# Output-weight sums held back during the last two phases of the first product group

## The chip, the cores and the metric

The kernel runs on one core of a Trainium2 chip. The number that counts is the time of one execution in microseconds (us) of device time. The kernel before was run three times; a fourth execution was recorded by the hardware profiler, and its trace is what the profile lines below come from. A core has five engines that follow their own instruction lists and wait for each other through semaphores: TensorE (PE in the profile, with its weight loads as PEld), VectorE (DVE), ScalarE (ACT), GpSimd (POOL) and SyncE (SP), which here issues the DMA transfers and computes nothing.

## The reference, cut to what matters

One layer of a hybrid encoder is computed for 1024 tokens of width 2048. One input projection produces everything that follows; one half of its columns feeds a sparse attention (an indexer scores all keys, each query keeps 256 of them), the other half a Mamba-2 state-space mixer (SSD) behind a short causal convolution. Both results are gated, concatenated and sent through one output projection; a residual and a layer norm close the layer.

```
u = einsum('bsd,de->bse', x, w_in)              # 1024 x 2048 x 6752
q, k, v, z_attn, q_idx, k_idx, w_idx, z_ssd, xbc, dt = split(u)
o_attn = sparse_attention(q, k, v, q_idx, k_idx, w_idx) * silu(z_attn)
o_ssd  = ssd_mixer(xbc, z_ssd, dt)              # conv, scan over chunks, gated RMS norm
mixed  = concatenate([o_attn, o_ssd])           # 1024 x 2048
sub    = einsum('bse,ed->bsd', mixed, w_out)    # 1024 x 2048 x 2048
out    = layer_norm(2 ** 0.25 * x + sub)
```

## The kernel before

**Matrix products.** All large products are float32 in effect: an operand is split into a high and a low part (names `xh` and `xl` for activations, `wh` and `wl` for weights), and three matmuls `xh*wh`, `xl*wh`, `xh*wl` replace one. The split of a weight tile is a pair of instructions: ACT rounds `wh<-wr`, DVE subtracts `wl<-wr,wh`. The same pair, `xh` and `xl`, makes an activation tile.

**Fewer products by Strassen-Winograd.** Both projections are done in 2x2 blocks with seven instead of eight block products, at the price of sums of operand blocks and of result blocks. For the input projection, pairs of column tiles go through such a scheme in two lists, the *product groups* (`PLAN`, `GROUPS`): the first has 8 pairs (keys, values, queries, a part of the SSD input), the second 14. Each group runs in four *phases* (`ph` 0 to 3 in `units`, line 600); a phase goes through all pairs of its group, two at a time, and phases 0 to 2 do so with two pieces for each pair (`f` 0 and 1). A *piece* is 24 matmuls of 512 columns into a PSUM bank `pj`. In phases 0 to 2 the second piece of a pair goes on accumulating on the bank of the first, after an engine has taken the intermediate result out of it: ACT copies it in phase 0 (`t_save`), DVE adds a loaded tile to it in phases 1 and 2 (`t_u`, `t_comb`; the row `u<-pj,u` or `cv<-pj,u`). That second piece cannot begin before (event `after`).

**Activation sets.** Each phase and each `f` multiplies by another set of eight tiles, loaded from DRAM (`xt`, or sums of its blocks, `xf`) and split by `t_xst`. A set can be split only when the tiles of the set two earlier become free, so at such a place eight ACT and eight DVE instructions come close together.

**Sums of the output weights.** For the output projection, four sums T1 to T4 of blocks of `w_out` are needed. They don't depend on the input, and `t_wsum` (line 837) makes them far ahead: 16 rounds, in two tasks of eight (one for each half of the columns). A round loads four 128x512 tiles from `wo` (256 KB each), makes four sums on DVE or GpSimd (`two` picks), and stores them to the DRAM tiles `ts`, 256 KB each. The output projection later loads them as `wr<-ts`.

**What sets the order.** The kernel is written by a planner that runs on the host while the program is built. Side work (everything but the pieces) is split into tasks, Python generators that stop at `Need(...)`: which engines the next step wants, which events, how many free slots of the tile pools (`u` has 29 slots, `keep=6` leaves six of them to others). Between small portions of the pieces, `pump` (line 482) goes through the tasks by priority and lets the first one that `ready` (line 436) accepts place its step. `ready` asks estimated clocks of the engines. So the places of all later instructions depend on what was placed before; a task that is held back leaves its place to others, and the order after it differs as well. Priority 0 belongs to what the pieces need, 5 to the weight sums.

Of the kernel before, what the change touches and what calls it, by code (L numbers as in the profile page):

```python
# [15 lines left out]
D = 2048  # L16
# [74 lines left out]
class Port:  # L91
# [3 lines left out]
    def __init__(self):  # L95
        self.busy = []
# [245 lines left out]


class Need:
    def __init__(self, eng="", ev=(), keep=0, now=False, late=0.0, **slots):
        self.eng, self.ev, self.slots, self.keep, self.now, self.late = eng, ev, slots, keep, now, late


# [7 lines left out]
class Flow:  # L356
# [6 lines left out]
    def __init__(self, nc):  # L363
        self.sim = Sim()
        self.nc = Engines(self, nc)
        self.clk = self.sim.clk
        self.cells = []
        self.tasks = []
        self.pool = {}
        self.slots = {}  # L370
        self.where = {}
        self.n = 0
        self.idle = 0.0
        self.idles = []
        self.spare = 2
        self.pressed = False
        self.first = ("kv10", "kv11", "kv00", "kv01")
        self.spare_u = 9
        self.signals = []
# [56 lines left out]
    def ready(self, task):  # L436
        n = task.need
        if "P" in n.eng:
            now = self.t - self.MARGIN
        else:  # L440
            now = max([self.t] + [self.clk[e] for e in n.eng or ("SP",)]) + 200.0
        late = 0.0 if self.pressed else n.late
        if task.ev.sure(late) + Sim.LAT > (self.t if n.now else now):
            return False
        for e in n.ev:
            if e.t is None or e.sure(late) > now:
                return False
        for tag, k in n.slots.items():
            if self.avail(tag) < k + (min(n.keep, self.spare_u) if tag == "u" else 0):
                return False  # L450
        slack = self.SLACK * (0.5 if task.prio >= 6 else 2 if task.prio == 0 else 1)
        return all(self.clk[e] <= self.t + slack for e in (n.eng or ("D" if task.prio >= 6 else "")) if e != "P")
# [126 lines left out]
class Layer:  # L579
# [20 lines left out]
    def units(self):  # L600

        pieces, work = [], []
        self.hooks = {}
        self.sets = []
        self.mate = {}

        def put(p, listed=True):
            if listed:
                work.append((len(pieces), None))
            pieces.append(p)  # L610
            return len(pieces) - 1

        def plain(h, tile, u, n):
            kind, j = tile
            t = ORDER.index(tile)
            p = Piece("T", h, t, u, load=(("w", t, u),), n=n + u, open=u == 0, close=u == 1, key=(h, t),
                      s0=256 if (kind == "qi" and h == 0) else 0)
            if u == 1:
                p.done = lambda ps: self.fl.add(getattr(self, "t_" + kind)(h, j, ps), 0, f"{kind}{j}h{h}", self.fl.t + 100)
            put(p)  # L620

        for pairs in PLAN:
            if isinstance(pairs, tuple):
                h, tiles, end = pairs
                n = len(self.sets)
                self.sets += [("x", h, 0), ("x", h, 1)]
                for part in [tiles[:3]] + [[t] for t in tiles[3:-end]] + [tiles[-end:]]:
                    for u in range(2):
                        for tile in part:
                            plain(h, tile, u, n)  # L630
                continue
            gi = GROUPS.index(pairs)
            if self.sets[-2:] != [("x", 0, 0), ("x", 0, 1)]:
                self.sets += [("x", 0, 0), ("x", 0, 1)]
            base = len(self.sets) - 2
            self.sets += [("f", "M2"), ("f", "M3"), ("f", "S1"), ("f", "S4"), ("x", 1, 1)]
            couples = [list(range(c, min(c + 2, len(pairs)))) for c in range(0, len(pairs), 2)]
            if len(couples[-1]) == 1:
                couples[-2:] = [couples[-2] + couples[-1]]
            for ph in range(4):  # L640
                for couple in [int(k) if k.isdigit() else k for k in OPENING] if (gi, ph) == (0, 0) else couples:
                    if isinstance(couple, str):
                        tile = ("misc", 0) if couple == "m" else QI["abcdefgh".index(couple)]
                        for u in range(2):
                            plain(0, tile, u, base)
                        continue
                    couple = couples[couple] if isinstance(couple, int) else couple
                    for f in range(1 + (ph < 3)):
                        for c in couple:
                            i = put(self.product(gi, c, pairs[c], ph, f, base + 2 * ph + f))  # L650
                            if f:
                                self.mate[gi, c, ph] = i
                            if ph and (ph, f) != (1, 1):
                                self.hooks.setdefault(max(i - 1, 0), []).append(lambda gi=gi, c=c, ph=ph, f=f: self.pre_ld(gi, c, ph, f))
        end = {}
        for i, p in enumerate(pieces):
            end[p.n] = i
        for i in end.values():
            pieces[i].last = True
        freed = sorted(end, key=end.get)  # L660
        for n in range(2, len(self.sets)):
            at = end[freed[n - 2]] - 2
            self.hooks.setdefault(at, []).append(lambda n=n: self.request(n))
        self.n_t = len(pieces)
        self.hooks.setdefault(self.n_t - 6, []).append(lambda: self.forms(0))
        self.hooks.setdefault(12, []).append(self.form_tasks)
        for half in range(2):
            self.hooks.setdefault(12, []).append(lambda half=half: self.fl.add(self.t_wsum(half), 5, "wsum"))
        for n in range(7):
            for d in range(2):  # L670
                for j in range(4):
                    if n < 6 or 4 * d + j < 8 - SKEW:
                        work.append((len(pieces), (0, 1, 2, 3)))
                    name = PRODUCTS[n][1]
                    pieces.append(Piece("O", n, d, j, load=(("o", name, d, j),)))
        for sts in ((0,), (1,), (2,), (3,)):
            work += [(len(pieces) - SKEW + j, sts) for j in range(SKEW)]
        return pieces, work
# [158 lines left out]
    def t_wsum(self, half):  # L837

        fl = self.fl
        cols = slice(512 * half, 512 * half + 512)  # L840

        def load(name, d, j):
            x = fl.new("us", [P, 512])
            fl.dma(x, self.w_block(name, d, j)[:, cols])
            return x

        def save(name, d, j, x):
            fl.dma(self.tsum[name, d, j][:, cols], x)
        for d in range(2):
            for j in range(4):  # L850
                yield Need("D", u=3, keep=6)
                x, y, z = load("B22", d, j), load("B12", d, j), fl.new("us", [P, 512])
                yield Need("V")
                fl.two(z, x, y, ALU.subtract)
                yield Need("")
                save("T3", d, j, z)
                fl.free(z)
                yield Need("D", us=1)
                z = load("B11", d, j)
                yield Need("V")  # L860
                fl.two(y, y, z, ALU.subtract)
                fl.free(z)
                fl.two(x, x, y, ALU.subtract)
                yield Need("D", us=1)
                save("T1", d, j, y)
                fl.free(y)
                save("T2", d, j, x)
                z = load("B21", d, j)
                yield Need("V")
                fl.two(z, x, z, ALU.subtract)  # L870
                fl.free(x)
                yield Need("")
                save("T4", d, j, z)
                fl.free(z)
                fl.signal(self.ev_wsum[half][4 * d + j])
# [1475 lines left out]
```

## Time and profile before

| | us |
|---|---|
| three runs | 1686.97, 1681.89, 1684.72 |
| median of the three | 1684.72 |
| the profiled execution, whole | 1679.99 |
| its span, first to last instruction | 1677.8 |
| PE busy in the span | 1622.1 (97%) |
| DVE busy | 1324.5 (79%) |
| ACT busy | 1002.2 (60%) |
| DMA, mean share of 16 engines | 71.2% (queue of SP) |

The span is that of one profiled execution; its whole time is 2.2 us longer than the span. In the rows, `out<-in` names what an instruction writes and reads, without the buffers' numbers; a number in square brackets is the idle time of the engine just before it and what ended that idle time. All instructions of the kernel carry the line of one helper (L312), so rows are told apart by tiles. SP rows are DMA issues: `u<-wo` a load, `ts<-u` a store. Matmul rows give a duration of 0.39 us, but they overlap: what counts is the distance from start to start, 0.227 us for 512 columns at full clock. The granted clock of PE is 1.00 or, after some idle stretches, 0.50.

By the order of the matmuls, the third phase of the first group begins at about 427 us of the span, its fourth at 526 us, and the second group at 571 us.

### The profile page before, as it was taken

How to read it: one execution, taken by the hardware profiler on the slowest of the kernel's cores; microseconds unless marked ns; L12 is line 12 of the kernel's file. 1: busy time of each engine (PE TensorE's matmuls, PEld its weight loads, DVE VectorE, ACT ScalarE, POOL GpSimd, SP SyncE). 2: the span in 40 equal slices, each digit the busy share in tenths (PEclk: the TensorE clock that was granted, in tenths of full speed). 3: DMA queues.
4: the chain of work that ended last, by engine and by line, in shares of the span. 5: the costliest groups of instructions: out<-in, count | busy, mean ns of one | idle time of the engine just before them, and what ended most of it. 6: DMA issues, size and time to landing. Idle time of an engine off the chain costs nothing. (4 is left out here: it accounts for less than half of the span.)

```text
span 1677.8 us, 23956 instructions
## 1 busy us (share of the span) xinstructions
PE 1622.1 (97%) x7996; PEld 1341.5 (80%) x7996; DVE 1324.5 (79%) x2437; ACT 1002.2 (60%) x1770; POOL 196.6 (12%) x212
## 2 busy tenths in 40 slices
PE   9999999999998999999999999999999999999997
PEld 6787787888786877888888877888787778888885
DVE  5889998998788876788686668785887676749998
ACT  4555666888877689774445356667757645532330
POOL 0000010000000000104133102312120001100110
PEclk9999999999999999999999999999999989999999
DMA  8177575789789767697684485466878979768654
GB/s 307 54 281 256 183 282 182 274 310 346 262 315 333 267 232 252 206 327 257 218 273 172 156 298 171 158 217 223 290 272 308 328 243 331 235 216 267 228 198 153
DMA packets 192643, 414.48 MB, mean 247 GB/s; under 512 B 19720, under 2 KB 56200, under 8 KB 192520
## 3 DMA queue, kind: packets, MB, share of 16 engines
q1 hardware_dynamic: 192088, 412.56, 71.2%
q8 instruction: 63, 1.03, 0.2%
q14 instruction: 60, 0.49, 0.1%
q10 hardware_dynamic: 432, 0.39, 0.1%
HBM read 308.94 MB, written 103.94 MB: 246 GB/s over the span
## 5 line engine op out<-in xcount | busy, mean ns | idle before, releaser
L312 PE MATMUL pj<-xh,wh 128*128 128x512 f32 (+1 forms) x1496 | 586.3, 392 | 23.2 <-DVE u L312 15.9
L312 PE MATMUL pj<-xh,wl 128*128 128x512 f32 (+1 forms) x1496 | 573.6, 383 | 3.4 <-DVE wl L312 3.4
L312 PE MATMUL pj<-xl,wh 128*128 128x512 f32 (+1 forms) x1496 | 573.3, 383 | 0.2 <-DVE xl L312 0.2
L312 DVE TENSOR_TENSOR wl<-wr,wh 128x1024 fp32r<-128x1024 f32 (+2 forms) x235 | 282.1, 1205 | 187.5 <-ACT wh L312 184.1
L312 PEld LDWEIGHTS pj<-xh,wh 128*128 128x128 f32 x1496 | 283.8, 190 | 78.9 <-issue 18.3
L312 PEld LDWEIGHTS pj<-xh,wl 128*128 128x128 f32 x1496 | 283.3, 189 | 60.9 <-DVE wl L312 5.3
L312 ACT ACTIVATE wh<-wr 128x1024 fp32r<-128x1024 f32 (+2 forms) x242 | 247.8, 1030 | 131.2 <-PE pj L312 100.0
L312 PEld LDWEIGHTS pj<-xl,wh 128*128 128x128 f32 x1496 | 283.9, 190 | 50.2 <-DVE xl L312 1.0
L312 PE MATMUL a<-u,u 128*128 128x512 f32 (+3 forms) x726 | 169.1, 352 | 3.9 <-DVE s L312 2.1
L312 PEld LDWEIGHTS a<-u,u 128*128 128x128 f32 x726 | 119.8, 189 | 37.6 <-DVE s L312 16.0
L312 ACT ACTIVATE u<-s,sm 128x640 bf16<-128x640 int16 (+7 forms) x132 | 129.6, 982 | 31.5 <-DVE sm L312 29.5
L312 DVE TENSOR_TENSOR u<-u,u 128x512 f32<-128x512 f32 (+5 forms) x215 | 139.1, 660 | 3.3 <-DMA u<-wo 0.8
L312 ACT ACTIVATE u<-a 128x512 fp32r<-128x512 f32 (+4 forms) x115 | 53.5, 481 | 147.4 <-PE a L312 74.5
L312 PE MATMUL pj<-wh,xh 128*128 128x512 f32 x318 | 129.5, 407 | 4.8 <-ACT xh L312 4.6
L312 PE MATMUL pj<-wh,xl 128*128 128x512 f32 x318 | 125.2, 394 | 0.1
L312 PE MATMUL pj<-wl,xh 128*128 128x512 f32 x318 | 125.0, 393 | 0.0
L312 ACT ACTIVATE a<-a 128x512 f32<-128x512 f32 (+3 forms) x160 | 77.1, 505 | 65.5 <-PE a L312 62.6
L312 ACT ACTIVATE u<-u 128x512 f32<-128x512 f32 (+4 forms) x147 | 80.6, 557 | 52.9 <-DVE u L312 47.2
L312 DVE TENSOR_TENSOR u<-pj,u 128x512 f32<-128x512 f32 (+2 forms) x112 | 74.6, 667 | 42.1 <-PE pj L312 39.2
L312 DVE TENSOR_TENSOR wr<-wr,wr 128x1024 f32<-128x1024 f32 x80 | 98.8, 1235 | 4.4 <-DMA wr<-wt 4.0
L312 POOL TENSOR_SCALAR s<-s,sm 128x640 f32<-128x640 f32 (+7 forms) x64 | 61.0, 966 | 207.7 <-DVE sm L312 152.5
L312 DVE SCALAR_TENSOR_TENSOR u<-cv,cw,u 128x512 f32<-128x512 f32 x96 | 72.3, 760 | 6.0 <-ACT u L312 3.7
(266 smaller groups left out, 2190.1 us busy)
## 6 DMA issues: line engine op xcount, KB each, us to landing
wr<-wt SPq DMA_DIRECT2D x187, 512.0 KB, 5.1
u<-u SPq DMA_DIRECT2D x110, 256.0 KB, 4.9
wr<-t SPq DMA_DIRECT2D x44, 512.0 KB, 7.6
wr<-ts SPq DMA_DIRECT2D x32, 512.0 KB, 4.9
u<-wo SPq DMA_DIRECT2D x63, 256.0 KB, 5.2
ts<-u SPq DMA_DIRECT2D x63, 256.0 KB, 4.9
s<-xt SPq DMA_DIRECT2D x24, 512.0 KB, 7.6
t<-wr SPq DMA_DIRECT2D x22, 512.0 KB, 2.8
```

Source lines behind the costliest of these rows:

```text
L312: f(*args, **kw)
```

## The change

`Need` gets a mark `rest`; the planner gets a switch `resting`, and `ready` refuses a step so marked while the switch is on. The first step of each round of the weight sums carries the mark. The switch goes on at the first piece of phase 2 (the third) of the first group and off at the first piece of the second group. A round that has begun goes on to its end; no new one begins in between.

```diff
 class Need:
-    def __init__(self, eng="", ev=(), keep=0, now=False, late=0.0, **slots):
+    def __init__(self, eng="", ev=(), keep=0, now=False, late=0.0, rest=False, **slots):
+        self.rest = rest
...
+        self.resting = False
...
     def ready(self, task):
...
+        if n.rest and self.resting:
+            return False
...
             for ph in range(4):
+                if (gi, ph) in ((0, 2), (1, 0)):
+                    self.hooks.setdefault(len(pieces), []).append(lambda on=gi == 0 and ph == 2: setattr(self.fl, "resting", on))
...
     def t_wsum(self, half):
...
-                yield Need("D", u=3, keep=6)
+                yield Need("D", u=3, keep=6, rest=True)
```

The program has as many DMA issues, matmuls and ACT instructions as before; DVE has eight instructions fewer and GpSimd three more; the planner picks the engine of some sums by its clocks. The first 2,088 rows of PE's order are the same; from there on tiles and places differ. By the end of the second group the tasks stand at other points too. Three places follow, each as it stood and as it stands; a name ends in its buffer's and its tile's number.

**SP's queue, about 450 us**, where the first round would have begun. `u<-wo` are loads of the weight sums and `ts` their stores, `u2`, `u3` and `t2` are intermediate results of the first group that come back, `wt` weights of the input projection. Before:

```order
L312 DMA k0_341<-u_806_4540 2x64x512
L312 DMA u_815_4666<-wo 128x512
L312 DMA u_816_4668<-wo 128x512
L312 DMA ts4_02_373<-u_807_4578 128x512
L312 DMA u_824_4705<-u3_0_3_4050 128x512
L312 DMA v0_1_344<-u_812_4595 128x512
L312 DMA u_825_4733<-wo 128x512
L312 DMA u_826_4735<-wo 128x512
L312 DMA wr_830_4742<-t2_0_5_4007 128x1024
L312 DMA wr_831_4743<-wt 128x1024
```

Now:

```order
L312 DMA k0_341<-u_806_4540 2x64x512
L312 DMA ts4_02_373<-u_807_4578 128x512
L312 DMA u_821_4700<-u3_0_3_4050 128x512
L312 DMA v0_1_344<-u_812_4595 128x512
L312 DMA wr_824_4732<-t2_0_5_4007 128x1024
L312 DMA wr_825_4733<-wt 128x1024
```

The four loads are gone from here; the store that remains ends a round begun earlier. From there to the beginning of the second group, ten loads and nine stores of the sums leave SP's queue, and the nine sums between them leave DVE's. The last store of a weight sum stands at place 623 of SP's list, where 582 was.

**DVE's list at the last set change of the third phase, about 508 to 519 us.** `xl` are the low parts of the new set, `wr<-wr,wr` sums of two weight tiles, `wl` the low part of a weight; the last row takes the intermediate result out of the bank of pair 7, and that pair's second piece waits for it. Before:

```order
L312 TENSOR_TENSOR xl_887_5168<-xr_871_5053,xh_886_5167 128x512
L312 TENSOR_TENSOR xl_889_5172<-xr_871_5053,xh_888_5171 128x512
L312 TENSOR_TENSOR wr_875_5093<-wr_875_5093,wr_876_5094 128x1024
L312 TENSOR_TENSOR xl_893_5187<-xr_872_5055,xh_892_5186 128x512
L312 TENSOR_TENSOR xl_895_5197<-xr_872_5055,xh_894_5196 128x512
L312 TENSOR_TENSOR xl_897_5201<-s4_873_5057,xh_896_5200 128x512
L312 TENSOR_TENSOR xl_899_5212<-s4_873_5057,xh_898_5211 128x512
L312 TENSOR_TENSOR xl_901_5216<-s4_874_5059,xh_900_5215 128x512
L312 TENSOR_TENSOR xl_903_5220<-s4_874_5059,xh_902_5219 128x512
L312 TENSOR_TENSOR wl_905_5224<-wr_864_4997,wh_904_5223 128x1024
L312 TENSOR_TENSOR wr_883_5156<-wr_883_5156,wr_884_5157 128x1024
L312 TENSOR_TENSOR u_880_5118<-pj_885_5160,u_880_5118 128x512
```

Now:

```order
L312 TENSOR_TENSOR xl_878_5141<-xr_862_5040,xh_877_5140 128x512
L312 TENSOR_TENSOR xl_880_5145<-xr_862_5040,xh_879_5144 128x512
L312 TENSOR_TENSOR xl_884_5159<-xr_863_5042,xh_883_5158 128x512
L312 TENSOR_TENSOR xl_886_5163<-xr_863_5042,xh_885_5162 128x512
L312 TENSOR_TENSOR wr_868_5083<-wr_868_5083,wr_869_5084 128x1024
L312 TENSOR_TENSOR xl_888_5174<-s4_864_5044,xh_887_5173 128x512
L312 TENSOR_TENSOR xl_890_5178<-s4_864_5044,xh_889_5177 128x512
L312 TENSOR_TENSOR xl_892_5188<-s4_865_5046,xh_891_5187 128x512
L312 TENSOR_TENSOR xl_894_5192<-s4_865_5046,xh_893_5191 128x512
L312 TENSOR_TENSOR wl_896_5197<-wr_856_4978,wh_895_5196 128x1024
L312 TENSOR_TENSOR wr_872_5117<-wr_872_5117,wr_873_5118 128x1024
L312 TENSOR_TENSOR u_871_5094<-pj_876_5133,u_871_5094 128x512
```

The same eight `xl`, two `wr` and one `wl` stand ahead of the last row; what differs is what comes before them in the list, from where the weight sums are gone.

**DVE's list at the last set change of the second group's third phase, about 1206 to 1212 us.** Before:

```order
L312 TENSOR_TENSOR xl_2244_12188<-xr_2205_12008,xh_2243_12187 128x512
L312 TENSOR_TENSOR xl_2246_12192<-xr_2205_12008,xh_2245_12191 128x512
L312 TENSOR_TENSOR wr_2212_12049<-wr_2212_12049,wr_2213_12050 128x1024
L312 TENSOR_TENSOR xl_2248_12203<-s4_2206_12010,xh_2247_12202 128x512
L312 TENSOR_TENSOR xl_2250_12207<-s4_2206_12010,xh_2249_12206 128x512
L312 TENSOR_TENSOR xl_2252_12217<-s4_2207_12012,xh_2251_12216 128x512
L312 TENSOR_TENSOR xl_2254_12221<-s4_2207_12012,xh_2253_12220 128x512
L312 TENSOR_TENSOR wr_2222_12114<-wr_2222_12114,wr_2223_12115 128x1024
L312 TENSOR_TENSOR wl_2259_12232<-wr_2198_11967,wh_2258_12231 128x1024
L312 TENSOR_TENSOR u_2196_11956<-u_2196_11956,u_2224_12124 128x512
L312 TENSOR_TENSOR u_2218_12086<-pj_2237_12159,u_2218_12086 128x512
```

Now:

```order
L312 TENSOR_TENSOR xl_2248_12208<-s4_2205_12017,xh_2247_12207 128x512
L312 TENSOR_TENSOR u_2193_11935<-u_2193_11935,u_2225_12110 128x512
L312 TENSOR_TENSOR u_2182_11876<-a_2250_12214,u_2182_11876 128x256
L312 SCALAR_TENSOR_TENSOR u_2175_11867<-u_2175_11867,dn_222,o_2251_12217 128x256 x2
L312 TENSOR_TENSOR xl_2256_12244<-s4_2206_12019,xh_2255_12243 128x512
L312 TENSOR_TENSOR xl_2258_12248<-s4_2206_12019,xh_2257_12247 128x512
L312 TENSOR_TENSOR wr_2230_12129<-wr_2230_12129,wr_2231_12130 128x1024
L312 TENSOR_TENSOR u_2224_12108<-pj_2235_12163,u_2224_12108 128x512
```

In both, the first row is the first that stands in the program behind the beginning of one piece, and the last is the row that the next piece waits for. Ahead of that last row there were six `xl`, two `wr` sums, a `wl` and a sum of another task; now there are three `xl`, one `wr` sum and four rows of other tasks. The other `xl` stand earlier, the `wl` and a `wr` sum behind.

## The prediction

> **What bounds the kernel now.** I read the page first, then the groups of instructions, then the timeline of PE at its long stops, then DVE, ACT and DMA around those.
>
> ```profile
> span 1677.8 us, 23956 instructions
> PE 1622.1 (97%) x7996; PEld 1341.5 (80%) x7996; DVE 1324.5 (79%) x2437; ACT 1002.2 (60%) x1770; POOL 196.6 (12%) x212
> ```
>
> TensorE is the bound: it is busy 97% of the span, so a change on other engines can give back only what PE loses in stops. The change doesn't touch PE's own work. The gain to be had is therefore read from the stops:
>
> ```profile
> 510.68 0.39 PE L312 MATMUL pj<-xl,wh 128*128 128x512 f32 x1
> 510.90 0.39 PE L312 MATMUL pj<-xh,wl 128*128 128x512 f32 x1
> 519.16 0.77 PE L312 MATMUL pj<-xh,wh 128*128 128x512 f32 x1 [7.87 <-DVE u L312]
> 519.72 0.63 PE L312 MATMUL pj<-xl,wh 128*128 128x512 f32 x1
> 520.15 0.63 PE L312 MATMUL pj<-xh,wl 128*128 128x512 f32 x1
> ...
> 523.06 0.40 PE L312 MATMUL pj<-xh,wh 128*128 128x512 f32 x1
> ...
> 632.56 0.80 PE L312 MATMUL pj<-xh,wh 128*128 128x512 f32 x1 [5.09 <-ACT u L312]
> 997.96 0.77 PE L312 MATMUL pj<-xh,wh 128*128 128x512 f32 x1 [3.11 <-DVE u L312]
> 1212.52 0.77 PE L312 MATMUL pj<-xh,wh 128*128 128x512 f32 x1 [3.15 <-DVE u L312]
> 1344.35 0.80 PE L312 MATMUL pj<-wh,xh 128*128 128x512 f32 x1 [4.64 <-ACT xh L312]
> ```
>
> These five stops, 23.9 us together, are PE's long ones (over 2 us) behind the change's beginning. Three wait for `DVE u`: a second piece cannot begin until DVE has taken the intermediate result out of its bank. A stop also costs clock: behind the one at 519 matmuls start 0.43 us apart (519.72 to 520.15) instead of 0.227, and nine of them start before 523.06, so it costs another 9 x 0.2 = 1.8 us. At 997.96 they start 0.43 apart as well; I put the loss there, and at 1212, at 1.3 us (six or seven matmuls).
>
> **The stop at 519, inside the rest.** These are rows of DVE's timeline up to the one that PE waits for (518.33):
>
> ```profile
> 496.92 1.23 DVE L312 TENSOR_TENSOR wr<-wr,wr 128x1024 f32<-128x1024 f32 x1 [2.60 <-DMA wr<-wt]
> ...
> 502.95 0.69 DVE L312 TENSOR_TENSOR u<-pj,u 128x512 f32<-128x512 f32 x1
> ...
> 507.36 1.23 DVE L312 TENSOR_TENSOR wl<-wr,wh 128x1024 fp32r<-128x1024 f32 x1 [3.38 <-ACT wh L312]
> 508.51 1.29 DVE L312 TENSOR_TENSOR xl<-xr,xh 128x512 fp32r<-128x512 f32 x2
> 510.85 1.23 DVE L312 TENSOR_TENSOR wr<-wr,wr 128x1024 f32<-128x1024 f32 x1 [1.05 <-DMA wr<-wt]
> 511.99 1.29 DVE L312 TENSOR_TENSOR xl<-xr,xh 128x512 fp32r<-128x512 f32 x2
> 513.19 2.49 DVE L312 TENSOR_TENSOR xl<-s,xh 128x512 fp32r<-128x512 f32 x4
> 515.60 1.22 DVE L312 TENSOR_TENSOR wl<-wr,wh 128x1024 fp32r<-128x1024 f32 x1
> 517.19 1.23 DVE L312 TENSOR_TENSOR wr<-wr,wr 128x1024 f32<-128x1024 f32 x1 [0.37 <-DMA wr<-wt]
> 518.33 0.68 DVE L312 TENSOR_TENSOR u<-pj,u 128x512 f32<-128x512 f32 x1
> ```
>
> And one of ACT's:
>
> ```profile
> 498.53 1.05 ACT L312 ACTIVATE u<-s,sm 128x896 bf16<-128x896 f32 x1 [2.30 <-DVE sm L312]
> ```
>
> DVE stood still 3.38 us for ACT's `wh`, and 1.05 and 0.37 us for weights. ACT was late because at 498.53 it had waited 2.30 us for DVE's small rows `sm` of the top-k search, and those stood behind the 2.60 us that DVE waited for a weight at 496.92. So a weight that lands late is passed on twice. Why late:
>
> ```profile
> wr<-wt SPq DMA_DIRECT2D x18, 512.0 KB, 9.2
> wr<-wt SPq DMA_DIRECT2D x187, 512.0 KB, 5.1
> L312 SPq DMA_DIRECT2D ts<-u x10: 320/326/453, 450.5 to 566.2; - x10
> L312 SPq DMA_DIRECT2D u<-wo x10: 328/457/1847, 447.9 to 532.6; - x10
> L312 SPq DMA_DIRECT2D wr<-ts x32: 319/320/1456, 1324.8 to 1534.8; - x32
> ```
>
> In 426 to 571 us a weight takes 9.2 us from issue to landing, in the whole span 5.1 (medians). The loads and stores of the sums are 20 of the transfers there, 256 KB each.
>
> **What the rest removes there.** Ten loads and nine stores: 19 x 0.262 = 5.0 MB. By the window rows below, 427 to 571 us carries 279 x 89 + 317 x 55 = 42.3 GB/s·us, or 42.3 MB, so 12% goes. Nine sums leave DVE, 9 x 0.60 = 5.4 us (rows of 128x512 follow each other at 0.60). Nothing on PE waits for them: the first is read at 1324.8.
>
> **Term 1: -5.3 us.** The rows ahead of the awaited one stay the same (eight `xl`, two `wr`, one `wl`). If the three waits of 3.38, 1.05 and 0.37 go, it comes 4.80 us earlier and PE stops 3.07 us. That is also what is left at 998 and 1212, where the same set change stands without late weights. Of the clock's 1.8 us, 1.3 stay: 4.8 + 0.5 = 5.3. Bounds: 9.7 (all 7.87 and 1.8, if the row at 502.95, which was late by the 2.60 too, moves up) and 0 (weights stay late, since the other 88% of the traffic stays).
>
> [...]
>
> **Where the moved sums go.** They start again at 571 us.
>
> ```profile
> core 0: us, PE busy (x) PEld busy (x) DVE busy (x) ACT busy (x) POOL busy (x), PEclk, DMA share, GB/s
> 427.00:516.00 89.00, 83.00 (x368) 67.74 (x366) 68.67 (x154) 74.76 (x140) 0.00 (x0) 1.00 0.80 279
> 516.00:571.00 55.00, 51.84 (x223) 42.81 (x224) 52.13 (x95) 33.82 (x58) 4.33 (x7) 0.94 0.87 317
> 571.00:700.00 129.00, 123.31 (x561) 101.16 (x559) 94.65 (x218) 110.49 (x206) 8.37 (x16) 0.99 0.72 246
> 700.00:830.00 130.00, 129.68 (x709) 110.98 (x708) 95.56 (x188) 79.01 (x146) 29.61 (x22) 1.00 0.73 253
> ```
>
> DVE has 34 us free in 571 to 700 and again in 700 to 830, and DMA 27%: 5.4 us and 5.0 MB hide there. **Term 2: 0.** Bounds 0 and +5.4 (all nine sums ahead of a row that PE waits for).
>
> **Term 3, the stop at 632: 0.** It is of another kind: ACT's copy out of a bank stands behind the SSD's decay group.
>
> ```profile
> 626.98 1.28 ACT L312 ACT_TABLE_LOAD   x1
> 628.27 1.28 ACT L312 ACTIVATE u<-s 64x512 f32<-64x512 f32 x2
> 629.58 2.44 ACT L312 ACTIVATE s<-s,ac 128x128 f32<-128x128 f32 x8
> 631.93 0.57 ACT L312 ACTIVATE u<-pj 128x512 f32<-128x512 f32 x1
> ```
>
> In the changed order the same eleven instructions stand three pieces earlier, again directly ahead of such a copy with one piece to go, with a `wh` and two top-k rows ahead of them. The stop moves to about 610 us; I leave its size. Bounds: gone with its clock, -6.4, or +3 (the rows ahead, 1.04 and twice about 0.9 us).
>
> **Terms 4 and 5, the set changes at 998 and 1212: -4.4 each.** For 1212, counted with the rows above: ahead of and with the awaited row stood, within one piece, six `xl` (0.60 each), two `wr` and a `wl` (1.14), one sum and the row itself (0.60): 8.2 us. A piece lasts 24 x 0.227 = 5.44, so 2.8 us too much; the stop was 3.15. Now three `xl`, one `wr`, four rows of other tasks and the row itself. At 0.60 for each of the four that is 5.9 us; three of them have half the width, and at 0.40 for these it is 5.3. The stop goes, and with it 1.3 of clock. At 998 it was six `xl`, two sums, a `wr`, a `wl` and the row, 7.7 us; now four `xl`, a row of half the width (0.40), a `wr` and the row, 4.5. Bounds for each: -4.4 and 0; at 998 ACT now has the decay group's 2.44 us ahead of the `xh`, which may hold the `xl` up.
>
> **Term 6, new stops: +4.4.** From 450 us on the order is another one. It was not made to remove the stops at 998 and 1212, and may make others. I count one of that kind and price. Bounds 0 and +13.2 (three).
>
> **Sum**: -5.3 + 0 + 0 - 4.4 - 4.4 + 4.4 = -9.7 us. The profiled execution took 1679.99 (span 1677.8 and 2.2 around it), so 1670.3; the median of the three runs lies 4.7 higher, and against it the forecast is 1684.7 - 9.7 = 1675.0.
>
> **Rivals.** *A, no difference.* Weights stay late (term 1 is 0), one of terms 4 and 5 fails, and the one new stop comes: 0 - 4.4 + 4.4 = 0, 1684.7. For it: 88% of the traffic stays, and ACT is busy 74.76 of 89 us there whatever DMA does. Against it: DMA and DVE both become lighter exactly where the waits are.
>
> *B, slower: side work comes late to the output projection.* The sums now take tile slots, DVE and SP in the second group, where attention and the SSD make what the output projection multiplies. Summing the changed order's rows with the durations above, DVE has about 11 us less work behind it than before when the output projection's fourth piece is placed. The stop at 1344 waits for such a late tile (`ACT xh`, 4.64). If the last tiles come 11 us later there, PE stops so much longer; from 5.3 us on this outweighs term 1. With terms 4 and 5 lost to new stops: 1684.7 - 5.3 + 11 = 1690.4. Against it: PE has other pieces there, and what is not done ahead of the output projection was not all needed by its first pieces.
>
> *C, the change doesn't do what it says*: the loads are out of SP's order, so this is as good as excluded; 1684.7.
>
> **How the numbers follow.** Forecast 0.57, A 0.24, B 0.17, C 0.02. A measurement of this kernel tells some 0.3% (5 us) from no change. The forecast's own range is 1666 to 1680: below, terms 1 and 3 go further (-4.4 and -5); above, half of it comes. The range for 8 in 10 leaves out most of B's far end: 1664 to 1689. Faster by over 0.3% (under 1679.7): the forecast, 0.57. Within: A and C and a small part of the forecast's shortfall, 0.26. Slower: B, 0.17.
>
> **What would show it.** In the changed profile: at the end of the first group's third phase a PE stop of about 3 us or less, and weights landing well under 9.2 us in 427 to 571 us (term 1); a stop behind `ACT u` near 610 us (term 3); no stop over 1 us at the set changes near 985 and 1200 us (4 and 5); DVE no fuller in 571 to 830 than 90% (term 2). I am wrong if weights land as late without the sums, if the stop at the third phase's end keeps over 6 us, or if the stop for `ACT xh` in the output projection grows by more than 5 us.

## The result and the profile after

The changed kernel takes 1665.0 us (median of 1661.71, 1664.92, 1665.08 and 1667.98), the kernel before 1684.11 us beside it (1681.89 to 1686.97). The ratio is 0.9885, 95% interval 0.9861 to 0.9909: faster by 19.1 us, where 9.7 were forecast. The direction was right, the size half; 1665.0 lies 1 us below the forecast's own range (1666 to 1680) and at the lower end of the wide one (1664 to 1689).

The profiled execution took 1667.98 us, three above its median; that of before (1679.99) lay four below its own. So the two traces differ by 7 us less than the medians. The page of after, its first lines:

```profile
span 1666.1 us, 23979 instructions
PE 1620.1 (97%) x7996; PEld 1340.9 (80%) x7996; DVE 1321.7 (79%) x2429; ACT 1002.0 (60%) x1770; POOL 197.3 (12%) x215
```

The span is 11.7 us shorter. PE's timeline of after at its stops from the change on (start, duration, instruction; in brackets the idle time before it and what ended it):

```profile
519.37 0.77 PE L312 MATMUL pj<-xh,wh 128*128 128x512 f32 x1 [4.89 <-DVE u L312]
...
544.57 0.50 PE L312 MATMUL pj<-xh,wl 128*128 128x512 f32 x1 [1.42 <-DVE wl L312]
...
585.73 0.50 PE L312 MATMUL pj<-xh,wh 128*128 128x512 f32 x1 [1.74 <-ACT u L312]
...
618.56 0.80 PE L312 MATMUL pj<-xh,wh 128*128 128x512 f32 x1 [4.31 <-ACT u L312]
...
1001.92 0.47 PE L312 MATMUL pj<-xh,wh 128*128 128x512 f32 x1 [1.56 <-ACT wh L312]
...
1279.40 0.61 PE L312 MATMUL a<-o,u 128*128 128x1 f32 x4 [1.48 <-DVE u L312]
```

Two of the five long stops of before are left: the one at the third phase's end (7.87, now 4.89) and the one behind the decay group (5.09 at 632, now 4.31 at 618). Of 3.11 at 998 half is left, with another releaser; the ones at 1212 and 1344 are gone. The last is the large one. The windows around it, before and then after:

```profile
core 0: us, PE busy (x) PEld busy (x) DVE busy (x) ACT busy (x) POOL busy (x), PEclk, DMA share, GB/s
1335.00:1345.00 10.00, 5.36 (x26) 3.95 (x24) 5.72 (x13) 6.97 (x16) 0.72 (x1) 0.86 0.82 281
1345.00:1355.00 10.00, 9.88 (x48) 7.80 (x46) 7.65 (x15) 2.34 (x4) 0.81 (x1) 0.63 0.44 141
```

```profile
1335.00:1345.00 10.00, 10.00 (x49) 8.33 (x48) 9.09 (x19) 4.88 (x9) 0.00 (x0) 1.00 0.69 236
1345.00:1355.00 10.00, 10.00 (x45) 8.26 (x44) 9.58 (x16) 8.59 (x18) 0.00 (x0) 1.00 0.99 339
```

Before, PE stood 4.64 us and then ran ten microseconds at a granted clock of 0.63, which costs another 10 x 0.37 = 3.7 us. After, it is never idle there and keeps its clock: 8.3 us, most of what the forecast lacks.

The four windows of the forecast, after:

```profile
427.00:516.00 89.00, 86.28 (x381) 70.20 (x380) 63.21 (x146) 77.96 (x148) 2.53 (x2) 1.00 0.74 259
516.00:571.00 55.00, 50.21 (x217) 40.84 (x218) 49.36 (x98) 37.86 (x69) 3.72 (x7) 0.97 0.85 311
571.00:700.00 129.00, 122.96 (x551) 100.68 (x549) 92.41 (x201) 104.88 (x189) 6.30 (x15) 0.97 0.67 229
700.00:830.00 130.00, 129.37 (x703) 110.51 (x703) 99.27 (x197) 77.29 (x140) 35.82 (x25) 1.00 0.78 272
```

DMA carries 259 instead of 279 GB/s up to 516 us; DVE is 72% and 76% busy where the moved sums run.

### The profile page after: what moved, and what is told of

It is laid out like the page before. It is cut to its first block, busy times and chain, and to the rows that moved or that the text cites. A ratio compares the mean times of both kernels' runs of the same rounds, so it can differ in the third digit from the quotient of the medians.

```text
span 1666.1 us, 23979 instructions
## 1 busy us (share of the span) xinstructions
PE 1620.1 (97%) x7996; PEld 1340.9 (80%) x7996; DVE 1321.7 (79%) x2429; ACT 1002.0 (60%) x1770; POOL 197.3 (12%) x215
## 5 line engine op out<-in xcount | busy, mean ns | idle before, releaser
L312 PE MATMUL a<-u,u 128*128 128x512 f32 (+3 forms) x736 | 172.8, 354 | 7.6 <-DVE s L312 4.4
L312 DVE TENSOR_TENSOR u<-u,u 128x512 f32<-128x512 f32 (+6 forms) x204 | 128.6, 645 | 5.7 <-DMA u<-wo 1.3
L312 PE MATMUL pj<-wh,xh 128*128 128x512 f32 x310 | 125.2, 404 | 0.5 <-DVE u L312 0.5
L312 PE MATMUL pj<-wh,xl 128*128 128x512 f32 x310 | 121.0, 390 | 0.0
L312 PE MATMUL pj<-wl,xh 128*128 128x512 f32 x310 | 121.0, 390 | 0.0
L312 DVE TENSOR_TENSOR wr<-wr,wr 128x1024 f32<-128x1024 f32 (+1 forms) x81 | 99.8, 1233 | 0.8 <-DMA wr<-wt 0.4
```

Of the source, the lines that this page charges most:

```text
L312: f(*args, **kw)
```

## The experiments

### Work or order: the sums left out of the old order, the work put back into the new one

The change does two things at once: it takes transfers and sums out of the third and fourth phase, and it gives everything behind 450 us another order. Two kernels separate them. In the first the planner plans the sums of that time as before, but they aren't issued:

```diff
+LEFT = ((0, 1, 0), (1, 0, 3), (0, 1, 1))
...
         def call(*args, **kw):
-            f(*args, **kw)
+            if not self.flow.ghost:
+                f(*args, **kw)
...
         def load(name, d, j):
             x = fl.new("us", [P, 512])
-            fl.dma(x, self.w_block(name, d, j)[:, cols])
+            with left(d, j, name):
+                fl.dma(x, self.w_block(name, d, j)[:, cols])
```

> The kernel before, every instruction in its old order; only the work of the sums between the first group's third phase and its end is left out (17 of its 19 transfers, since two loads come back at 571 us, and nine sums on DVE), and the output weights that would need them are read from another place, so the output is not the layer's. Theory 'relief' (the time was won where traffic and DVE were relieved): most of the 19 us are found here, 1684 to 1672 or less. Theory 'order' (relief is worth only what it does to the stop at 519; the far stops differ because the planner placed other work otherwise): the stop at 519 falls from 7.87 to about 4.9 us and its half clock from 6.8 to 3.4 us, which makes some 4.5 us, 1679 to 1680; the stops at 632, 998, 1212 and 1344 stay as they were, within 0.5 us each.

In the second, transfers and DVE rows of the same number and size are added to the changed kernel at the places where before has them (`EXTRA`), without the planner's knowledge (the loads here go from one place in memory to another):

```diff
                 fl.pump()
+                self.extra(EXTRA.get((i, q), ""))
...
+            if kind == "V":
+                self.nc.vector.engine.tensor_tensor(out=self.spill, in0=c[0], in1=c[1], op=ALU.subtract)
+            else:
+                self.nc.sync.engine.dma_start(self.scratch(f"extra{n}", [P, 512]), self.w_block("B22", n % 2, n % 4)[:, 0:512])
```

> The changed kernel, every instruction in its order, with ten loads, nine stores (here 19 transfers of 256 KB from one place in memory to another) and nine DVE subtractions of 128x512 added at the pieces of the third and fourth phase where the kernel before has them. Relief: the gain is gone, 1665 to 1680 or more. Order: the stop at 519 grows again by some 3 us with its clock, 4.5 us in all, 1669 to 1670, and the stops at 632, 998, 1212 and 1344 stay away.

| | work as before | work taken out |
|---|---|---|
| order of before | 1 | 0.9985 (0.9976 to 0.9994) |
| order of the changed kernel | 0.9921 (0.9909 to 0.9934) | 0.9885 (0.9861 to 0.9909) |

In microseconds (times 1685): the relief alone is worth 2.5, the new order alone 13.3, both together 19.4. In the new order the relief is worth 6.1; that difference is known to some 4.5 us, so the 3.6 between 6.1 and 2.5 are not clear of noise. PE's timeline of the kernel with the sums left out:

```profile
518.04 0.77 PE L316 MATMUL pj<-xh,wh 128*128 128x512 f32 x1 [6.24 <-DVE u L316]
...
631.36 0.80 PE L316 MATMUL pj<-xh,wh 128*128 128x512 f32 x1 [5.12 <-ACT u L316]
...
997.22 0.69 PE L316 MATMUL pj<-xh,wh 128*128 128x512 f32 x1 [3.12 <-DVE u L316]
...
1212.04 0.50 PE L316 MATMUL pj<-xh,wh 128*128 128x512 f32 x1 [3.15 <-DVE u L316]
...
1344.74 0.80 PE L316 MATMUL pj<-wh,xh 128*128 128x512 f32 x1 [4.64 <-ACT xh L316]
```

All stops but the first are those of before to 0.03 us: they belong to the order, not to the load. With the work put back into the new order only one of the five returns, the stop at the third phase's end:

```profile
521.31 0.77 PE L315 MATMUL pj<-xh,wh 128*128 128x512 f32 x1 [7.95 <-DVE u L315]
```

So 'order' holds, though it had put the relief at 4.5 us in place of 2.5. In the new order this stop hangs on the load (7.95 with it, 4.89 without). Why the relief gave only 1.6 us of it in the old order is in DVE's rows of the kernel with the sums left out:

```profile
506.69 1.23 DVE L316 TENSOR_TENSOR wl<-wr,wh 128x1024 fp32r<-128x1024 f32 x1 [3.38 <-ACT wh L316]
...
510.19 1.23 DVE L316 TENSOR_TENSOR wr<-wr,wr 128x1024 f32<-128x1024 f32 x1 [1.07 <-DMA wr<-wt]
```

The two larger of the three waits, 3.38 and 1.05, are still there, one of them to the hundredth.

### Rows exchanged at one stop

If a stop is set by what stands ahead of the awaited row in its engine's list, exchanging those rows and nothing else must remove it. `AFTER_COPY` names the SSD's decay groups that are issued only after the next awaited copy or `xh`:

```diff
+AFTER_COPY = ((100, 0, 0, 0), (192, 1, 1, 0),)
...
         def call(*args, **kw):
-            f(*args, **kw)
+            if self.flow.holding:
+                self.flow.held.append(lambda kw=dict(kw): f(*args, **kw))
+            else:
+                f(*args, **kw)
...
+            fl.holding = (fl.piece, h, g, cp) in AFTER_COPY
             for q in range(2):
```

> The kernel before with two places of ACT's order changed and nothing else: at 632 us the awaited copy u<-pj goes ahead of the decay group (table load, two 64x512, eight 128x128), and at 1344 us the awaited xh with the four rows before it goes ahead of the second decay group (two 64x512, eight 128x128). Order: both stops are a matter of what stands ahead on ACT; the one at 632 goes (5.09 us and 1.6 of clock), the one at 1344 falls from 4.64 to 1 or 2 us and its 10.2 us of half clock go: 11 to 14 us in all, 1670 to 1673. Rival (the stops only move, because DVE and PE wait for the decay group a piece later): under 5 us, 1680 or more.

Measured: 0.9976 (0.9967 to 0.9984), 1680.1 us: 4 us, a miss. At 632 the stop went, but PE met 1.34 us at 637 and 1.72 us at 674, and of the 5 us gained there 4 were lost again by 680 us: the rival holds there. At 1344 the stop is still 2.92 us. ACT's rows say why:

```profile
1341.92 0.28 ACT L318 ACTIVATE xl<-a 128x128 f32<-128x128 f32 x1 [1.43 <-DVE u L318]
1342.10 1.05 ACT L318 ACTIVATE s<-s 128x1024 f32<-128x1024 f32 x1
1343.04 1.05 ACT L318 ACTIVATE wh<-wr 128x1024 fp32r<-128x1024 f32 x1
1343.99 0.62 ACT L318 ACTIVATE xh<-xh 128x512 fp32r<-128x512 f32 x1
```

With the decay group out of the way, another task's copy stood ahead of the awaited `xh` and itself waited 1.43 us. What is late is the place of `xh` in the list, not one row ahead of it.

The same exchange in the changed kernel, at 618 (`AFTER_COPY = ((97, 0, 0, 0),)`):

> The changed kernel with one place of ACT's order changed: at 618 us the awaited copy u<-pj goes ahead of the decay group's eleven rows. Order: the stop of 4.31 us goes with its half clock of 6.8 us, 6 to 8 us, 1657 to 1659. Rival (the group is late for what follows, and the stop comes back a piece later): under 3 us, 1662 or more.

Measured: 0.9874 (0.9859 to 0.9889), 1662.0 us, 3 us under the changed kernel's median, half of the 6 to 8 expected and not clear of noise (the changed kernel: 0.9861 to 0.9909). In the trace the stop is gone, and the mean granted clock of the execution is 0.993 where it was 0.992; the span is 5.7 us shorter.

### The late tile at 1344

The eighth pair `xh`, `xl` of the output projection's first product is placed by the old order at the beginning of the piece that needs it, and by the new one four pieces sooner. This kernel gives the old order the new place, by refusing steps of the SSD until the pair is placed:

```diff
+        if self.hold and task.name.startswith("ssd"):
+            return False
...
+        self.hooks.setdefault(self.n_t - 3, []).append(lambda: setattr(self.fl, "hold", True))
...
         raw = self.raws.pop((n, kk))
+        fl.hold = fl.hold and (n, kk) != (0, 7)
```

> The kernel before, its order kept up to the last three pieces ahead of the output projection; from there no step of the SSD is placed until the last of the eight tiles that the output projection's first product multiplies has been put on ACT and DVE. That tile then stands at the beginning of the last piece ahead of the output projection (as in the changed kernel) instead of at the beginning of the output projection's fourth piece, which needs it. Theory 'late tile': the stop of 4.64 us at 1344 and its 10.2 us of half clock are the price of that tile's place, and go: 9 to 12 us, 1673 to 1676; the stops at 519, 632, 998 and 1212 stay as they were. Rival (the SSD is late in its turn and PE stops for it further on): under 4 us, 1681 or more.

Measured: 1.0006 (0.9995 to 1.0017). The theory is refuted, the rival holds: the stop of 4.64 is gone, but PE stops for other late work further on and loses as much again:

```profile
1358.01 0.50 PE L312 MATMUL a<-wh,xh 128*128 128x512 f32 x1 [2.17 <-DVE sm L312]
...
1380.80 1.09 PE L312 MATMUL o<-s,u 128*64 128x128 f32 x16 [1.21 <-DVE u L312]
...
1462.12 0.50 PE L312 MATMUL pj<-wh,xl 128*128 128x512 f32 x1 [1.81 <-DVE xl L312]
```

### Other orders, with and without the rest

Is the new order good because of the rest, or by luck? `SLACK` says how many ns an engine's list may be planned ahead of PE (2650). Changed by a little from the third phase on, it gives another order without touching the sums. Five values, each without the rest (this diff on the kernel before) and with it (on the changed kernel):

```diff
             for ph in range(4):
+                if (gi, ph) == (0, 2):
+                    self.hooks.setdefault(len(pieces), []).append(lambda: setattr(self.fl, "SLACK", 2640.0))
```

> The kernel before with nothing changed about the sums: from the first group's third phase on the planner's allowance for work ahead of PE is 2640 in place of 2650 ns, so that the order becomes another one by chance. Theory 'chance of order' (the stops at 998, 1212 and 1344 are accidents of the order before, and most other orders lack some of them): from the rows on DVE and ACT the stops at 519 and 632 stay, the one at 998 goes (4.4), the one at 1212 shrinks to about 1 us (3), the tile of 1344 is placed at the end of the last piece ahead of the output projection and its stop goes (9 to 12): 1665 to 1669. Rival (the rest of the sums, not the order, is what frees those places): no change beyond 5 us, 1680 or more.

> As the run with 2640, with 2700 ns. Chance of order: from the rows the stops at 519 (9 with its clock), 998, 1212 (4.4 each) and 1344 (9 to 12) go, the one at 632 moves a piece on and becomes 2 us longer (2): 1656 to 1661. Rival: no change beyond 5 us, 1680 or more.

> One of three kernels that with the earlier ones make pairs with and without the rest, each pair at the same allowance (2600, 2640, 2650, 2700 ns) from the third phase on. This one: no rest, 2600. Theory 'chance of order': the orders without the rest lie around 1685 with a scatter of some 5 us, so 1680 to 1690; that the rest won 19 us at 2650 is mostly that order's luck. Rival 'the rest wins everywhere': without the rest 1680 to 1690 too; it is the other kernels of the pairs that tell them apart.

> The rest, with 2600. Chance of order: within 8 us of its partner without the rest, either sign, some 3 us better on average (what relief alone gave). The rest wins everywhere: 12 us or more better than its partner, 1674 or less.

> The rest, with 2640; its partner without the rest took 1684.9. Chance of order: 1677 to 1690. The rest wins everywhere: 1673 or less.

> The rest, with 2700; its partner without the rest took 1683.5. Chance of order: 1676 to 1689. The rest wins everywhere: 1671 or less.

> No rest, allowance 2660. So far four kernels without the rest (2600, 2640, 2650, 2700) took 1683.5 to 1685.4, their partners with it 1668.1, 1676.2, 1665.3, 1677.2. Theory 'the rest orders better' (without it the orders are all about as good as the one before; with it they are better by 6 to 19): 1682 to 1687. Rival 'small sample': the orders without the rest scatter too, this one may lie at 1675 or less.

> The rest, allowance 2660. The rest orders better: 6 to 19 us under its partner, 1665 to 1678. Small sample: within 5 us of its partner or above it.

> No rest, allowance 2750. The rest orders better: 1682 to 1687. Small sample: anywhere from 1670 to 1690.

> The rest, allowance 2750. The rest orders better: 6 to 19 us under its partner. Small sample: within 5 us of its partner or above it.

Ratios to the kernel before, with the medians in us:

| SLACK | no rest | rest | difference, us |
|---|---|---|---|
| 2600 | 0.9993 (1683.5) | 0.9903 (1668.1) | -15.2 |
| 2640 | 0.9997 (1684.9) | 0.9952 (1676.2) | -7.6 |
| 2650 | 1 (1684.1) | 0.9885 (1665.0) | -19.4 |
| 2660 | 0.9992 (1683.4) | 0.9954 (1676.9) | -6.4 |
| 2700 | 0.9985 (1683.5) | 0.9961 (1677.2) | -4.0 |
| 2750 | 1.0043 (1692.1) | 0.9944 (1674.6) | -16.7 |

(The difference is that of the ratios times 1685; each ratio is known to 0.1% to 0.2%, the one at 2650 to 0.24%.) The rest is faster in all six pairs, by 4 to 19 us, 11.5 on average; the smallest difference, 4.0 at 2700, is known to 3 us. So neither theory holds as it was put: the gain is no accident of one order, but its size is, and the pair that was asked about has the largest.

The forecasts for 2640 and 2700 without the rest (1665 to 1669, 1656 to 1661) were made by adding up the stops of the old order that the new rows would remove. They were off by 18 and 24 us, though most of those stops did go or shrink (left are 2.19 near 1200 at 2640 and 3.84 near 516 at 2700): other ones came. At 2640 PE's and DVE's rows:

```profile
1437.95 0.98 PE L312 MATMUL a<-o,u 128*128 128x1 f32 x4 [6.33 <-DVE u L312]
```

```profile
1435.05 1.22 DVE L312 TENSOR_TENSOR wl<-wr,wh 128x1024 fp32r<-128x1024 f32 x1 [4.66 <-ACT wh L312]
```

Here two decay groups stand on ACT around a weight's `wh`, DVE waits for that with its `wl`, and the row that PE needs is behind it.

Where does the rest gain on average? PE's idle time, added up over its rows, falls from 46.6 us (mean of the six without) to 37.6: 1.8 us less in the third phase, 4.4 less in the second group, 2.9 less in the output projection. Half speed behind the stops costs some 2 us less besides, counted as half of PE's busy time at a granted clock of 0.50. Most of it is won where the rest has long ended, and none of these three places has it in more than four of the six pairs.

### The rest's length

The changed kernel with the rest ended one phase sooner, and one phase later:

```diff
-                if (gi, ph) in ((0, 2), (1, 0)):
+                if (gi, ph) in ((0, 2), (0, 3)):
```

```diff
-                if (gi, ph) in ((0, 2), (1, 0)):
+                if (gi, ph) in ((0, 2), (1, 1)):
```

> The changed kernel with the rest ended at the beginning of the first group's fourth phase instead of the second group (a rest in the fourth phase alone leaves the order of the kernel before as it was, so the third phase is where the rest acts). Chance of order: the stop at 519 is as in the changed kernel (4 us better than before), none near 618 or 632 (6), none at 998 (4.4), the one at 1212 is there as before, none at 1344 (9 to 12): 1659 to 1662. Relief (the longer the sums rest, the more is won): between the two kernels, 1670 to 1680.

> The changed kernel with the rest kept up through the first phase of the second group (it ends where the second phase begins). Theory 'the rest orders better, by keeping the sums behind the tasks that are needed sooner': a longer rest keeps the gain, 1660 to 1675. Rival 'the gain hangs on the length that was chosen': as with the rest in the third phase alone (1689), 1682 or more.

Measured: 1.0028 (1.0012 to 1.0044) for the shorter, 1.0131 (1.0109 to 1.0152) for the longer, 1689.2 and 1709.8 us. Both theories failed on the shorter one (1659 to 1662 and 1670 to 1680 were expected). The longer one is 22 us slower: 'the rest orders better' failed there (1660 to 1675), and the rival, that the gain hangs on the length that was chosen, holds (1682 or more). The longer rest's stores of sums, and PE's stops behind them:

```profile
L312 SPq DMA_DIRECT2D ts<-u x5: 319/418/1172, 1349.7 to 1450.2; - x5
```

```profile
1426.72 0.98 PE L312 MATMUL a<-o,u 128*128 128x1 f32 x4 [4.33 <-DVE u L312]
...
1456.54 0.79 PE L312 MATMUL pj<-wh,xh 128*128 128x512 f32 x1 [5.25 <-ACT wh L312]
```

The last sum is stored at 1450 us, inside the output projection, whose next product can't load its weight before. Meanwhile PE has only side work, and its clock falls; the window 1425 to 1475 of that kernel, and then of the changed one:

```profile
1425.00:1475.00 50.00, 36.32 (x178) 29.44 (x179) 31.64 (x67) 26.63 (x57) 6.97 (x7) 0.69 0.69 228
```

```profile
1425.00:1475.00 50.00, 50.00 (x264) 41.58 (x263) 33.57 (x59) 25.69 (x43) 6.65 (x5) 1.00 0.53 180
```

That is rival B's kind of loss (side work late to the output projection), at a rest one phase longer. Why the shorter rest is slower than none is not settled; no sum is late there, and its largest stops behind the rest (4.75 at 1200, 6.47 at 1448 for `ACT xh`) are of the kind that any order can have.

### Rows exchanged at four stops of the changed kernel

As above at 618, and three more exchanges of the same make: each holds the rows ahead back until the awaited one is issued.

```diff
+        if i == 86:
+            fl.hold(("comb", 0, 7, 2, 0))
         fl.two(x, x, parts[1], p.op)
...
+                    if fl.piece == 92 and not self.ev_after(1, 0, 0).cells:
+                        fl.holding = fl.held_for = ("save", 1, 0)
                     fl.act(junk[:, 0:(i + 1) * P], src, AF.Sign, bias=bias[:, j:j + 1], accum_out=count[:, j:j + 1])
...
+        if kp == 3:
+            fl.hold("split")
         fl.two(d, d, c, ALU.add)
```

> The changed kernel with rows exchanged at its four largest stops and nothing else: at 618 the copy u<-pj ahead of the decay group (as in the run with one row ahead, 1662.0); at 585 the copy u<-pj ahead of two top-k rows (1.7 us of ACT); at 519 the awaited u<-pj ahead of a weight's sum (1.2 us of DVE and its wait of 0.4); at 290 the two awaited wl ahead of a row that waits 3 us for its load. If each stop is set by what stands ahead in its engine's queue: 1.7 + 1.6 + 2.5 and some clock less than 1662.0, 1655 to 1658. Rival (PE meets the next row of the same queue and stops there): 1660 or more.

Measured: 0.9827 (0.9808 to 0.9846), 1658.2 us (1657.17 to 1658.6), 0.2 us above what was expected (1655 to 1658) and clear of the rival's 1660; 29 us under the kernel before and the fastest of all. Its page, and its largest stop:

```profile
span 1656.1 us, 23979 instructions
PE 1616.9 (98%) x7996; PEld 1336.5 (81%) x7996; DVE 1319.0 (80%) x2429; ACT 1002.4 (61%) x1770; POOL 199.1 (12%) x215
```

```profile
514.31 0.47 PE L315 MATMUL pj<-xh,wh 128*128 128x512 f32 x1 [3.63 <-DVE u L315]
```

## Why the prediction was right in direction and half in size

**The bound** (PE, through its stops) was right: PE's work is the same, and its idle time and clock carry the whole difference.

**Term 1, the stop at 519, -5.3: too large, and the reason half wrong.** The stop lost 2.98 us where 4.80 were forecast; 4.89 are left, not 3. Behind it seven matmuls start 0.43 us apart (519.37 to 522.07) where nine did, which is another 0.4: -3.4. Of the three waits of DVE the largest did not go. The rows of after:

```profile
509.17 1.23 DVE L312 TENSOR_TENSOR wl<-wr,wh 128x1024 fp32r<-128x1024 f32 x1 [4.08 <-ACT wh L312]
...
516.26 1.22 DVE L312 TENSOR_TENSOR wl<-wr,wh 128x1024 fp32r<-128x1024 f32 x1
517.40 1.23 DVE L312 TENSOR_TENSOR wr<-wr,wr 128x1024 f32<-128x1024 f32 x1
518.54 0.68 DVE L312 TENSOR_TENSOR u<-pj,u 128x512 f32<-128x512 f32 x1
```

The waits for weights (1.05 and 0.37) went, the 3.38 for `wh` became 4.08. My step that ACT was late because a weight had been late is wrong: ACT was full. Between one `wh` and the next it runs top-k rows back to back, from 502.04 to 508.09 us, without a wait, as it did before from 501.33 to 506.29; and with the sums left out of the old order the wait of 2.60 fell to 1.43, while the 3.38 stayed. What made up the 2.98 are the two waits (1.4) and an earlier start of the chain against PE (1.4): PE comes to this stop 3.2 us later in the trace of after (514.48, before 511.29), the `wl` at 509.17 only 1.8 us later. ACT's rows of after:

```profile
501.09 1.04 ACT L312 ACTIVATE wh<-wr 128x1024 fp32r<-128x1024 f32 x1
502.04 0.81 ACT L312 ACTIVATE u<-s,sm 128x640 bf16<-128x640 f32 x1
...
508.09 1.04 ACT L312 ACTIVATE wh<-wr 128x1024 fp32r<-128x1024 f32 x1
```

A landing time of the weights, which I had named as a sign, isn't given for after; what DVE waits for them is, in the whole span 4.0 us before and 0.4 after (groups of the two pages):

```profile
L312 DVE TENSOR_TENSOR wr<-wr,wr 128x1024 f32<-128x1024 f32 x80 | 98.8, 1235 | 4.4 <-DMA wr<-wt 4.0
```

```profile
L312 DVE TENSOR_TENSOR wr<-wr,wr 128x1024 f32<-128x1024 f32 (+1 forms) x81 | 99.8, 1233 | 0.8 <-DMA wr<-wt 0.4
```

**Term 2, the moved sums, 0**: right, DVE stays at 72 and 76%. **Term 3, 0**: nearly right; the stop moved to 618 (forecast near 610), 0.8 shorter, but the half speed behind it lasts 6.0 us where it lasted 3.0, which costs 1.5: +0.7.

**Terms 4 and 5, -4.4 each**: the one at 1212 came as forecast; at 998 the forecast row is in time, but `ACT wh` now keeps PE 1.56 us. Together -7.2 (4.4, and 1.55 with its 1.3 of clock).

**Term 6, new stops, +4.4**: stops of 1.42 and 1.74 us came, 1.56 at 1048 and 0.91 at 1203 went, and the one at 1279 is 0.35 shorter than its like before (1.83 at 1278) but now costs 3.4 us of half speed, 1.7: about +2.

Up to here the terms measure -3.4 + 0.7 - 7.2 + 2 = -7.9, not far from the forecast's -9.7. **The step that failed is what the sum lacks: no term for the output projection.** I quoted the stop at 1344 as one of PE's five long ones and then left it out of the sum as unchanged; only rival B spoke of it, and with the wrong sign. B read "11 us less DVE work behind it" as side work that comes late; in fact the awaited tile stands four pieces sooner, and the stop with its clock, 8.3 us, is gone. -7.9 - 8.3 = -16.2. The two traces differ by 15.5 us behind 427 us (11.7 in their spans, and after comes to this point 3.8 us later, mostly by a stop near 231 us that is told below); the 19.1 of the medians hold 3.6 us more, which these two traces don't show.

That sum is bookkeeping after the event, though, and the experiments keep it from being a rule: with the tile alone moved the time stayed (1.0006), and two sums of the same make for other orders missed by 18 and 24 us. What is shown: the order carries 13 of the 19 us, the relief 2.5 in the old order and 6.1 in the new; the rest, at this length, is faster in six orders of six, by 11.5 us on average; this pair lies at the favourable end, by luck of its order. What stays open is by what the rest makes better orders, since most of it is won far behind it, and why a rest of one phase doesn't.

**Rival A** (weights stay late, no difference) didn't come, though in the old order it nearly held: one of the waits for weights stayed (1.07), and the gain was 2.5 us. **B** didn't come, but its mechanism is real and 22 us dear at a rest of two phases and one more. **C** was rightly excluded.

## What to carry to other kernels

When a planner sets the order, a small change to one task reorders everything behind it. Separate the two with a kernel of the old order without the work and one of the new order with the work put back; then repeat the change in a few neighbouring orders before its gain is called its own. A list of stops that go is no forecast: ask at each of PE's long stops, the far ones too, what else is queued in front of the awaited row. Rows exchanged by hand at the stops that are left, with the rest of the order kept, came closer to their forecast in the changed kernel (7 us by four exchanges, 0.2 us from the range) than in the kernel before (4 us of 11 to 14).

## What the runs showed of the hardware that I had not expected

Short stops cost clock or don't, with no threshold to be seen in their length in the traces of before and after. PE's rows of after behind the stop of 1.74 us before 585.73 (starts 0.23 apart, full speed) and behind the one of 1.48 us before 1279.40 (0.43 apart, half):

```profile
586.06 0.39 PE L312 MATMUL pj<-xl,wh 128*128 128x512 f32 x1
586.29 0.40 PE L312 MATMUL pj<-xh,wl 128*128 128x512 f32 x1
...
1280.38 0.63 PE L312 MATMUL pj<-xl,wh 128*128 128x512 f32 x1
1280.81 0.63 PE L312 MATMUL pj<-xh,wl 128*128 128x512 f32 x1
```

The share of idle time around a stop doesn't tell the two apart either. The 3.4 us that hold the end of the stop of 1.74 us, those that hold the stop of 1.48 us, and the 3.4 us behind these:

```profile
core 0: us, PE busy (x) PEld busy (x) DVE busy (x) ACT busy (x) POOL busy (x), PEclk, DMA share, GB/s
583.61:587.03 3.42, 1.69 (x8) 1.08 (x7) 3.35 (x6) 2.98 (x8) 0.00 (x0) 1.00 0.53 199
1276.52:1279.93 3.41, 1.94 (x12) 1.32 (x10) 3.38 (x8) 0.29 (x2) 0.00 (x0) 1.00 1.03 395
1279.93:1283.34 3.41, 3.41 (x12) 2.83 (x11) 2.06 (x5) 2.64 (x5) 0.00 (x0) 0.50 1.06 404
```

The first is idle for half of its time and keeps the clock. The second is idle for 43%, has 0.5 us of one-column matmuls besides, and behind it PE is granted 0.50 until 1283.3, for 3.4 us. What makes the difference is not shown. Up to PE's last instruction the half-speed stretches of after begin at 232.0, 293.5, 518.8, 617.8 and 1279.9 us; the one at 617.8 lasts 6.8 us, the others 3.4 each.

Executions also differ by a stop. The longest wait of PE's `a` matmuls for `DVE s` is 2.0 or 2.1 us in four profiled executions (after, 2600 with the rest and without, 2700 with it) and 0.8 in seven (before, 2640 with and without, 2700 without, the SSD held, the shorter and the longer rest). In after it stands near 231 us, in the part that the change doesn't touch and where before has the same order. With its clock the stop costs 2.9 us here: after's matmuls come 0.6 us later than before's ahead of it, 3.4 behind it. Why it comes in some executions is not shown:

```profile
231.73 1.88 PE L312 MATMUL a<-u,u 128*128 128x512 f32 x4 [2.01 <-DVE s L312]
```
